# Two-bank projections of a hybrid diffusion layer: token columns cut 320 + 320 where they were cut 384 + 256

## The chip, the cores and the metric

The kernel runs on one core of one Trainium2 chip. The time is device microseconds of one execution. Three runs of the kernel before have a median of 982.79 us (981.87, 982.79, 984.15). The profile is of one execution on the same kind of chip, and lists each instruction by engine: TensorE (PE for the matmuls, PEld for the loads of their weights), VectorE (DVE), ScalarE (ACT), GpSimd (POOL) and SyncE (SP), whose queue issues the transfers.

## The reference

One layer of a bidirectional diffusion backbone is applied to 512 latent and 128 context tokens of 1024 channels. All arithmetic is float32. What matters of it:

```python
h = rms_norm(x, norm_mix_pre) * (1 + sc1) + sh1
proj = h @ w_in                                   # 1024 -> 4640 columns
#   ... Mamba-2 scan in both directions on one part, a 31-tap convolution module on the other
mix = concatenate([y_ssd, u]) @ w_out             # 2048 -> 1024
x = x + g1 * rms_norm(mix, norm_mix_post)
h = rms_norm(x, norm_ffn_pre) * (1 + sc2) + sh2
up = h @ w_ffn_up                                 # 1024 -> 5632
up = dwconv(up)                                   # 3x3 on the latent grid, width 3 on the context
f = (silu(f_gate) * f_val) @ w_ffn_down           # 2816 -> 1024
x = x + g2 * rms_norm(f, norm_ffn_post)
```

The four products with `w_in`, `w_out`, `w_ffn_up` and `w_ffn_down` are the projections. Nearly all of the time goes into them.

## The kernel before

**Layout.** Channels lie on the 128 partitions and tokens along the free dimension: 512 latent tokens and then 128 context tokens, 640 in all (`T`). A projection takes one block of 128 output channels at a time. It sums over blocks of 128 input channels into a tile of PSUM with 1024 float32 columns, which is two banks of 512 (`psum`, `next_ps`, tiles `ps` in the profile; three of them rotate). Small one-bank tiles (`psq`, `pq` in the profile) serve the sums of the norms, the scan and some halves.

**Three products for one.** Weights and inputs are each split into a high part of a reduced float32 format and a remainder (`hi` and `lo`; `wh` and `wl` for weights). `mm3` adds three products for each block of input channels: high weights by high input, high weights by the input's remainder, and the remainder of the weights by high input. 640 columns do not fit into one bank, so each product is two matmuls, one for each half of the tokens, with the same weights, one after the other. Every matmul has its own load of weights. All matmuls of `mm3` are recorded on one line, L415.

**The halves.** `HC` cuts the tokens into 0 to 384 and 384 to 640. `HALF` puts the first half at column 128 of the tile, so that it ends with the first bank at 512, and the second half at column 512. A reader takes both as one stretch of 640 columns through `view`, which begins at column 128.

The same halves order the work around the norms. Before the FFN's first norm and at the end of the kernel, the last output blocks are summed for tokens 0 to 384 first and for 384 to 640 after that, so that the norm of one half runs under the matmuls of the other. In the output projection, blocks 3 to 7 (`OUT_FULL` is 3) go by halves, blocks 0 to 2 take all tokens. In the up projection the first five blocks (`HEAD`) go by halves through `up_mm` (L1259), the other 39 take all tokens through `mm3`. In the down projection block 0 takes all tokens, but its two halves go to two one-bank tiles (`places`); blocks 1 to 6 take all tokens in a two-bank tile; and block 7 goes by halves. All blocks of the input projection take all tokens.

**Order.** The program is recorded as plain Python, and then `issue_in_order` puts each engine's instructions into an order written out as a table of numbers (`ORDER`). The matmuls of a block of output channels therefore mostly stand together on TensorE, but before 540 us two or three blocks, the scan's small matmuls (L744, L807, L818) and the adaLN's (L441, L460) are interleaved.

**What reads the sums.** `out_done` (L1072) adds a stored part to the output projection's sums; `up_conv_of` (L1327 is one call of it) runs a 3x3 convolution of a block on VectorE out of PSUM (L1237); `down_out` (L1407) squares and scales the down projection's sums on ScalarE. In the input projection, ScalarE and VectorE read the tile through `view` as well. Weights come by 512 KB transfers on SyncE's queue, are rounded to `wh` on ScalarE (L311) and their remainder `wl` is made on GpSimd (L313).

Of the kernel before, what the change touches and what calls it, by code (L numbers as in the profile page):

```python
# [11 lines left out]
MUL, ADD, SUB, MAX, MIN = ALU.mult, ALU.add, ALU.subtract, ALU.max, ALU.min  # L12
# [5 lines left out]
T = L + C  # L18
HT = T // 2
HC = ((0, 384), (384, T))  # L20
NCH = T // P
KD = D // P
NPAIR = 8
# [160 lines left out]
def hybrid_layer_kernel(ctx: ExitStack, tc: tile.TileContext, xT, ct, prm, cst, wrest, wdt, idhl_d, wada1, wada2, win,  # L184
                        wout, wup, wdown, st0, yT, nsf, nsb):
    nc = tc.nc
    te, ve, ac, gp, sy = nc.tensor, nc.vector, nc.scalar, nc.gpsimd, nc.sync
# [17 lines left out]
    def nm(s):  # L205
        uid[0] += 1
        return f"{s}_{uid[0]}"


    def slot(tag, dt=F32, shape=(P, T)):  # L210
        if tag in ("H8", "T8"):
            return sb.tile([P, T + 64], dt, tag=tag, name=nm(tag))[:, 48:48 + shape[1]]
        return sb.tile(list(shape), dt, tag=tag, name=nm(tag))
# [4 lines left out]
    def psq(i):  # L218
        return ps.tile([P, 512], F32, tag=f"Q{i}", name=nm(f"pq{i}"))

    def view(t):
        return t[:, 128:128 + T]

    def prm_col(name, i=0, n=1):
        a = _COLS[name][0] + i
        return prms[:, a:a + n]
# [5 lines left out]
    for k in range(KD):  # L232
        t = slot(f"T{k}")
# [147 lines left out]
    ups = [(q, half) for q in range(NF) for half in range(2)]  # L381
# [21 lines left out]
        return hi, lo  # L403

    last_mm = [None]
    HALF = ((128, *HC[0]), (512, *HC[1]))

    def mm3(pt, hi, lo, j, xh, xl, first, last, halves=(0, 1), places=None):
        w1 = hi[:, j * P:(j + 1) * P]
        w2 = lo[:, j * P:(j + 1) * P]  # L410
        for i, (w, x) in enumerate(((w1, xl), (w1, xh), (w2, xh)) if first else ((w1, xh), (w1, xl), (w2, xh))):
            for h in halves:
                o, c0, c1 = HALF[h]
                out = places[h] if places else pt[:, o:o + c1 - c0]
                last_mm[0] = te.matmul(out, w, x[:, c0:c1], start=first and i == 0, stop=last and i == 2)  # L415

# [136 lines left out]
    def proj(n):  # L553
        (u,) = unit_of[n]
        hi, lo = get_unit(u)
        pt = psum(flip[0] % 2)
        flip[0] += 1
        for k in range(KD):
            mm3(pt, hi, lo, k, h_hi[k], h_lo[k], k == 0, k == KD - 1)
        return pt  # L560
# [23 lines left out]
    def chunked(t):  # L584
        return t.rearrange("p (c t) -> p c t", c=NCH)

# [9 lines left out]
    def dtprep():  # L596
# [5 lines left out]
        pd = psq(0)  # L602
        for c in range(NCH):
            te.matmul(pd[:, c * 32:(c + 1) * 32], raw[:, c * P:(c + 1) * P], ids, start=True, stop=True)
        W = NCH * 32
        scr = slot("T9")
        a, n, e, w = (scr[:, i * W:(i + 1) * W] for i in range(4))
        by = lambda t: t.rearrange("p (c h) -> p c h", c=NCH)
        ve.tensor_tensor(by(a), by(pd[:, 0:W]), prm_col("dt_bias", 0, 32).unsqueeze(1).to_broadcast([P, NCH, 32]), ADD)
        ve.scalar_tensor_tensor(n, a, -1.0, a, MUL, MAX)  # L610
        ac.activation(e, n, AF.Exp, scale=-1.0)

        DT = slot("T12")[:, 0:W].rearrange("p (c h) -> p c h", c=NCH)
        ve.tensor_scalar(n, e, 2.0, None, ADD)
# [235 lines left out]
    def gate(p, pg):  # L850
        for (o0, o1), (c0, c1) in UCOLS:
            ac.activation(ub[p % 3][:, o0:o1], view(pg)[:, c0:c1], AF.Tanh, scale=0.5)
# [74 lines left out]
    for it in seq:  # L927
        if it[0] == "proj":
            n = it[1]
            pt = proj(n)  # L930
# [61 lines left out]
    ahead_sb = [None] * KD  # L992
# [45 lines left out]
    def next_ps():  # L1038
        rot[0] += 1
        return psum(rot[0] % 3)  # L1040

    BOTH = (0, 1)
    RANGES = (((0, *HC[0]),), ((0, HC[1][0], L), (1, L, T)))

    def cols_of(halves):
        return slice(HC[halves[0]][0], HC[halves[-1]][1])

    def ranges_of(halves):
        return ((0, 0, L), (1, L, T)) if len(halves) == 2 else RANGES[halves[0]]
# [17 lines left out]
    def out_done(m, halves, pt):  # L1067
        if m_sb[m] is None:
            m_sb[m] = slot(f"M{m}")
        cc = cols_of(halves)  # L1070
        o = m_sb[m][:, cc]
        ve.tensor_tensor(o, view(pt)[:, cc], ahead_sb[m][:, cc], ADD)  # L1072
        if m == 0:
            ac.activation(msq[:, cc], o, AF.Square)
            return
        sq = slot(f"S{16 + m % 2}")
        ac.activation(sq[:, cc], o, AF.Square)
        if m < KD - 1:
            gp.tensor_tensor(msq[:, cc], msq[:, cc], sq[:, cc], ADD)
        else:  # L1080
            sq_last[halves[0]] = sq
# [17 lines left out]
    def xr_fetch():  # L1099
        for k in range(KD):  # L1100
            t = slot(f"T{8 + k}")
            sy.dma_start(t[:, slice(*HC[0])], xT[:, k, slice(*HC[0])])
            xr[0].append(t[:, slice(*HC[0])])

# [28 lines left out]
    class Mid:  # L1133
        def __init__(self, half):
            self.half, (self.c0, self.c1) = half, HC[half]
            self.n = self.c1 - self.c0
            self.t = {}
# [70 lines left out]
    for half in range(2):  # L1208
        for m in range(OUT_FULL, KD):
            pt = next_ps()  # L1210
# [14 lines left out]
    def up_conv(v, i, out):  # L1225
        w = lambda a, b: prm_col("ffn_w", 9 * i + 3 * a + b)
        ac.activation(out, v, AF.Identity, bias=prm_col("ffn_b", i), scale=w(1, 1))  # L1227
        vl = v[:, 0:L].rearrange("p (r c) -> p r c", c=GW)
        ol = out[:, 0:L].rearrange("p (r c) -> p r c", c=GW)
        for a in range(3):  # L1230
            for b in range(3):
                if (a, b) == (1, 1):
                    continue
                r0, r1 = max(0, 1 - a), min(ROWS, ROWS + 1 - a)
                q0, q1 = max(0, 1 - b), min(GW, GW + 1 - b)
                ob = ol[:, r0:r1, q0:q1]
                ve.scalar_tensor_tensor(ob, vl[:, r0 + a - 1:r1 + a - 1, q0 + b - 1:q1 + b - 1],  # L1237
                                        w(a, b), ob, MUL, ADD)
        ve.scalar_tensor_tensor(out[:, L + 1:T], v[:, L:T - 1], w(1, 0), out[:, L + 1:T], MUL, ADD)
        return ve.scalar_tensor_tensor(out[:, L:T - 1], v[:, L + 1:T], w(1, 2), out[:, L:T - 1], MUL, ADD)  # L1240
# [4 lines left out]
    for i in range(KD // 2):  # L1245
        t = sb.tile([P, 2, HC[1][1] - HC[1][0]], F32, tag=f"H{i}", name=nm("xr"))
        sy.dma_start(t, xT[:, 2 * i:2 * i + 2, slice(*HC[1])])
        xr[1] += [t[:, 0, :], t[:, 1, :]]
    head = [next_ps() for i in range(3)]
# [6 lines left out]
    def up_mm(i, k, half, pt, o):  # L1256
        (hi, lo), (c0, c1) = ws[i], HC[half]
        for j, (w, x) in enumerate(((hi, h2[k][0]), (hi, h2[k][1]), (lo, h2[k][0]))):
            te.matmul(pt[:, o:o + c1 - c0], w[k] if i in (1, 2) else w[:, k * P:(k + 1) * P], x[:, c0:c1],  # L1259
                      start=k == 0 and j == 0, stop=k == KD - 1 and j == 2)  # L1260
        if k == KD - 1 and i >= 3:
            ac.activation(raws[i][:, c0:c1], pt[:, o:o + c1 - c0], AF.Copy)
# [48 lines left out]
    def up_conv_of(i, v, out):  # L1311
        conved[i] = out
        prior[0] = up_conv(v, ups[i][1] * NF + ups[i][0], out)

    acc_slot = lambda q, half: slot({(1, 0): "S16", (2, 1): "S17"}.get((q, half), f"S{10 + 2 * half + q % 2}"))
    ada_half(6, ada_w2)
    for i in (0, 3, 4, 1, 2):
        if i >= 3:
            pt = psq((i + 1) % 2)
            for k in range(KD):  # L1320
                up_mm(i, k, 1, pt, 0)
            horizon[0] += 1
            fetch(horizon[0])
            continue
        for k in range(KD):
            up_mm(i, k, 1, head[i], 512)
        up_conv_of(i, view(head[i]), acc_slot(*ups[i]))  # L1327
    horizon[0] = None
    FRAW = [f"H{i}" for i in (2, 3, 4, 7, 0, 1, 8, 9, 10, 11, 12, 13, 14, 15, 5, 6)] + ["S8", "S9"]

# [11 lines left out]
    for i in range(HEAD, 2 * NF):  # L1342
        q, half = ups[i]
        w = get_unit(unit_of["up", i])
        pt = next_ps()
# [56 lines left out]
    def down_out(m, half, pt):  # L1402
        halves = BOTH if half is None else (half,)
        if mg[m] is None:
            mg[m] = slot(mtags[m])
        cc = cols_of(halves)
        v = zero_at[half] if m == 0 else view(pt)[:, cc]  # L1407
        if m == 0:
            ac.activation(msq[:, cc], v, AF.Square)
        else:  # L1410
            sq = sq_last[0] if half else slot("AT" if m % 2 else "HL")
            ac.activation(sq[:, cc], v, AF.Square)
            if half is None:
                gp.tensor_tensor(msq[:, cc], msq[:, cc], sq[:, cc], ADD)
            else:
                sq_last[half] = sq
        for c, c0, c1 in ranges_of(halves):
            ac.activation(mg[m][:, c0:c1], v[:, c0 - cc.start:c1 - cc.start], AF.Copy, scale=gg2[:, m, c:c + 1])
# [32 lines left out]
    zero_at = [psq(h)[:, 0:HC[h][1] - HC[h][0]] for h in range(2)]  # L1451
# [7 lines left out]
    for m in range(2, KD - 1):  # L1459
        pt = next_ps()  # L1460
        down_mm(m, None, pt, range(NF))
        down_out(m, None, pt)

    m = KD - 1
    pt = next_ps()
    down_mm(m, 0, pt, range(NF))
    down_out(m, 0, pt)
    pt = next_ps()
# [128 lines left out]
```

## Time and profile before

| | |
|---|---|
| median of three runs | 982.79 us |
| span of the profiled execution | 979.4 us |
| TensorE busy (7623 matmuls) | 944.5 us, 96% |
| weight loads busy (7623) | 920.9 us, 94% |
| VectorE, ScalarE, GpSimd busy | 686.9, 471.3, 577.9 us |
| matmuls of L415 | 5424: 2712 of 384 columns, 2712 of 256 |
| mean granted TensorE clock | 0.996 of full speed |
| moved from and to memory | 117.5 MB, mean 120 GB/s |

The page gives the profiled execution's span, from its first to its last instruction; it does not give that execution's time from the outside. A matmul's duration in the profile (332 to 337 ns for 384 columns, 279 to 282 for 256) is longer than the distance to the start of the next one, because matmuls overlap in the pipeline. What a stream of matmuls costs is read from the starts, or from a stretch of the chain of waits with its count. Rows of the timeline merge successive matmuls on the same tiles whatever their width, and name the width of the first.

### The profile page before, as it was taken

To read this page: it belongs to the slowest core of one execution; us is meant where nothing else is said; L and a number is where in the kernel's file an instruction comes from. 1 tells how busy PE (TensorE), PEld (TensorE's weight loads), DVE (VectorE), ACT (ScalarE), POOL (GpSimd) and SP (SyncE) were. 2 spreads that over 40 slices of the span, in tenths; PEclk is the share of its full clock that TensorE was granted. 3 is DMA by queue.
4 is the path that set the end of the run, shared out by engine and by line. 5 is a ranking of instruction groups with operands and counts; after the bars stand their busy time and mean duration, and the time that the engine had idled before them with its cause. 6 is when DMAs were issued, how large, how long until landed. Compare 5 with 4: busy or idle time off the path is not lost.

```text
span 979.4 us, 18795 instructions
## 1 busy us (share of the span) xinstructions
PE 944.5 (96%) x7623; PEld 920.9 (94%) x7623; DVE 686.9 (70%) x1076; ACT 471.3 (48%) x799; POOL 577.9 (59%) x416
## 2 busy tenths in 40 slices
PE   4999999999999999999999999999999999999995
PEld 3799999999999998998889999999999999999995
DVE  1769898999989997523585998998988898400004
ACT  4355666877668477622464852323232336322211
POOL 1334699889999882534662994444454436543434
PEclk9999999999999999999999999999999999999998
DMA  9622424433424422578662322222222231322213
GB/s 347 250 72 86 117 82 127 146 95 123 139 80 142 128 91 93 196 244 303 200 218 88 129 86 69 84 78 73 86 66 86 66 87 54 94 69 76 82 38 108
DMA packets 50294, 117.52 MB, mean 120 GB/s; under 512 B 6016, under 2 KB 13952, under 8 KB 50208
## 3 DMA queue, kind: packets, MB, share of 16 engines
q1 hardware_dynamic: 50208, 116.33, 37.2%
q8 instruction: 60, 0.98, 0.4%
q14 instruction: 26, 0.21, 0.1%
HBM read 112.55 MB, written 3.75 MB: 119 GB/s over the span
## 4 chain that ended last, share of the span: by engine, by line
PE 87%; DMA 3%; ACT 3%; DVE 2%; SPq 1%; POOL 1%; issue 1%; POOLq 0%; ACTq 0%; DVEq 0%
PE ps L415 72%; PE ps L1259 3%; PE pq L415 2%; PE pq L818 2%; PE pq L807 1%; PE pq L460 1%; SPq L452 1%; DMA wr<-in_wout 1%; PE pq L744 1%; PE pq L441 1%; POOL wl L313 1%; PE pq L473 1%; DMA S<-acD 1%; ACT wh L311 1%; DMA T<-in_wada 1%
## 5 line engine op out<-in xcount | busy, mean ns | idle before, releaser
L313 POOL TENSOR_TENSOR wl<-wr,wh 128x1024 fp32r<-128x1024 f32 (+3 forms) x127 | 290.4, 2290 | 316.3 <-ACT wh L311 299.2
L415 PE MATMUL ps<-H,wh 128*128 128x384 f32 (+1 forms) x1636 | 315.7, 309 | 0.1
L311 ACT ACTIVATE wh<-wr 128x1024 fp32r<-128x1024 f32 (+3 forms) x131 | 131.3, 1003 | 316.2 <-PE ps L415 183.2
L415 PE MATMUL ps<-T,wh 128*128 128x384 f32 (+1 forms) x1472 | 272.5, 306 | 1.8 <-ACT S L1227 1.8
L1237 DVE SCALAR_TENSOR_TENSOR S<-ps,prms,S 128x441 f32<-128x441 f32 (+2 forms) x336 | 233.5, 695 | 29.4 <-ACT S L1227 18.9
L415 PEld LDWEIGHTS ps<-H,wh 128*128 128x128 f32 x1636 | 249.0, 188 | 2.7 <-issue 1.7
L415 PEld LDWEIGHTS ps<-T,wh 128*128 128x128 f32 x1472 | 218.9, 188 | 2.2 <-ACT S L1227 2.1
L872 DVE SCALAR_TENSOR_TENSOR ps<-u,prms,ps 128x655 f32<-128x655 f32 x205 | 185.1, 903 | 10.8 <-ACT ps L869 4.8
L415 PE MATMUL ps<-H,wl 128*128 128x384 f32 (+1 forms) x818 | 191.8, 309 | 0.0
L415 PE MATMUL ps<-T,wl 128*128 128x384 f32 (+1 forms) x736 | 166.2, 305 | 0.0
L415 PEld LDWEIGHTS ps<-H,wl 128*128 128x128 f32 x818 | 129.0, 188 | 1.0 <-issue 1.0
L415 PEld LDWEIGHTS ps<-T,wl 128*128 128x128 f32 x736 | 113.0, 188 | 0.0
L488 DVE RECIPROCAL rsm<-rsm 128x160 f32<-128x160 f32 (+2 forms) x9 | 7.4, 817 | 147.1 <-ACT rsm L487 147.1
L415 PE MATMUL ps<-S,wh 128*128 128x384 f32 (+1 forms) x420 | 88.0, 310 | 1.6 <-ACT wh L311 1.6
L415 PEld LDWEIGHTS ps<-S,wh 128*128 128x128 f32 x420 | 66.5, 188 | 2.8 <-ACT wh L311 1.8
L415 PE MATMUL ps<-S,wl 128*128 128x384 f32 (+1 forms) x210 | 54.9, 309 | 0.3 <-POOL wl L313 0.3
L789 ACT ACTIVATE S<-S,AC 128x128 f32<-128x128 f32 x140 | 45.5, 392 | 2.4 <-DMA S<-acD 2.4
L885 POOL TENSOR_TENSOR T<-T,T 128x640 f32<-128x640 f32 x20 | 32.0, 1602 | 12.5 <-ACT T L881 12.5
L1227 ACT ACTIVATE S<-ps,prms 128x640 f32<-128x640 f32 x42 | 36.5, 869 | 0.0
L415 PEld LDWEIGHTS ps<-S,wl 128*128 128x128 f32 x210 | 35.2, 188 | 0.9 <-POOL wl L313 0.5
L881 ACT ACTIVATE T<-u,prms 128x512 f32<-128x512 f32 (+1 forms) x54 | 27.9, 554 | 6.8 <-POOL T L885 6.8
L1339 POOL TENSOR_TENSOR H<-S,S 128x640 f32<-128x640 f32 x16 | 25.3, 1581 | 0.0
(346 smaller groups left out, 1180.3 us busy)
## 6 DMA issues: line engine op xcount, KB each, us to landing
wr<-in_wup SPq DMA_DIRECT2D x44, 512.0 KB, 3.5
wr<-in_win SPq DMA_DIRECT2D x36, 512.0 KB, 3.9
T<-in_wada SPq DMA_DIRECT2D x49, 256.0 KB, 5.4
S<-acD SPq DMA_DIRECT2D x28, 320.0 KB, 4.7
wr<-in_wdown SPq DMA_DIRECT2D x16, 512.0 KB, 3.4
wr<-in_wout SPq DMA_DIRECT2D x13, 512.0 KB, 4.5
H<-in_wada SPq DMA_DIRECT2D x23, 256.0 KB, 4.6
S<-in_wada SPq DMA_DIRECT2D x16, 256.0 KB, 5.4
```

The costliest lines, as they stand in the source:

```text
L311: ac.activation(hi[:, :n], raw[:, :n], AF.Copy)
L313: lo_eng.tensor_tensor(lo[:, :n], raw[:, :n], hi[:, :n].bitcast(F32), SUB)
L415: last_mm[0] = te.matmul(out, w, x[:, c0:c1], start=first and i == 0, stop=last and i == 2)
L789: ac.activation(rc, rc, AF.Relu, scale=-1.0, bias=AC2[:, c, row:row + 1])
L818: te.matmul(py[64 * h:64 * h + 64, i * P:(i + 1) * P], xt[:, c * P + 64 * h:c * P + 64 * h + 64], rs[h, d][:, c * P:(c + 1) * P], start=d ...
L872: ve.scalar_tensor_tensor(acc, u[:, j:j + UO], w(j), acc, MUL, ADD)
L881: ac.activation(t[:, b:c], u[:, a:a + c - b], AF.Copy, scale=w(j))
L885: gp.tensor_tensor(far, far, t, ADD)
L1227: ac.activation(out, v, AF.Identity, bias=prm_col("ffn_b", i), scale=w(1, 1))
L1237: ve.scalar_tensor_tensor(ob, vl[:, r0 + a - 1:r1 + a - 1, q0 + b - 1:q1 + b - 1], w(a, b), ob, MUL, ADD)
L1259: te.matmul(pt[:, o:o + c1 - c0], w[k] if i in (1, 2) else w[:, k * P:(k + 1) * P], x[:, c0:c1], start=k == 0 and j == 0, stop=k == KD - 1 ...
L1339: gp.tensor_tensor(f_raw[q], a, b, MUL)
```

## The change

Where `mm3` sums all tokens in one two-bank tile, it cuts the 640 columns into 0 to 320 and 320 to 640. The first half is put at column 192, so that it still ends with the first bank, and the second at 512 (`EVEN`). `view` begins at 192 for such a tile and at 128 for one that is summed by halves; its callers say which. Tiles that are summed by halves, the one whose halves go to two one-bank tiles, and `up_mm` keep 384 and 256. The norms' halves (`HC`) stay.

```diff
 HC = ((0, 384), (384, T))
+HALF = ((128, *HC[0]), (512, *HC[1]))
+EVEN = ((512 - T // 2, 0, T // 2), (512, T // 2, T))
...
-    def view(t):
-        return t[:, 128:128 + T]
+    def view(t, even=True):
+        o = EVEN[0][0] if even else HALF[0][0]
+        return t[:, o:o + T]
...
-    HALF = ((128, *HC[0]), (512, *HC[1]))

     def mm3(pt, hi, lo, j, xh, xl, first, last, halves=(0, 1), places=None):
         w1 = hi[:, j * P:(j + 1) * P]
         w2 = lo[:, j * P:(j + 1) * P]
+        cuts = EVEN if len(halves) == 2 and not places else HALF
         for i, (w, x) in enumerate(((w1, xl), (w1, xh), (w2, xh)) if first else ((w1, xh), (w1, xl), (w2, xh))):
             for h in halves:
-                o, c0, c1 = HALF[h]
+                o, c0, c1 = cuts[h]
                 out = places[h] if places else pt[:, o:o + c1 - c0]
                 last_mm[0] = te.matmul(out, w, x[:, c0:c1], start=first and i == 0, stop=last and i == 2)
...
-        ve.tensor_tensor(o, view(pt)[:, cc], ahead_sb[m][:, cc], ADD)
+        ve.tensor_tensor(o, view(pt, len(halves) == 2)[:, cc], ahead_sb[m][:, cc], ADD)
...
-        up_conv_of(i, view(head[i]), acc_slot(*ups[i]))
+        up_conv_of(i, view(head[i], False), acc_slot(*ups[i]))
...
-        v = zero_at[half] if m == 0 else view(pt)[:, cc]
+        v = zero_at[half] if m == 0 else view(pt, len(halves) == 2)[:, cc]
```

The order of instructions stays the same on every engine, and so do the waits between them. On TensorE, 4830 of the 5424 matmuls of `mm3` get another width: 2415 of 384 and 2415 of 256 columns become 4830 of 320. One place in the up projection, the first blocks of input channels of one block of outputs (`ps0` is the PSUM tile, `T` are inputs, `wh77` and `wl77` the weights' two parts; the size is partitions by columns), before:

```order
L415 MATMUL ps0_705_7018<-T8_600_5820,wh77_6825 128x384
L415 MATMUL ps0_705_7018<-T8_600_5820,wh77_6825 128x256
L415 MATMUL ps0_705_7018<-T0_599_5819,wh77_6825 128x384
L415 MATMUL ps0_705_7018<-T0_599_5819,wh77_6825 128x256
L415 MATMUL ps0_705_7018<-T0_599_5819,wl77_6827 128x384
L415 MATMUL ps0_705_7018<-T0_599_5819,wl77_6827 128x256
```

and after the change (two matmuls of one row now have the same size):

```order
L418 MATMUL ps0_705_7018<-T8_600_5820,wh77_6825 128x320 x2
L418 MATMUL ps0_705_7018<-T0_599_5819,wh77_6825 128x320 x2
L418 MATMUL ps0_705_7018<-T0_599_5819,wl77_6827 128x320 x2
L418 MATMUL ps0_705_7018<-T1_602_5824,wh77_6825 128x320 x2
L418 MATMUL ps0_705_7018<-T9_603_5825,wh77_6825 128x320 x2
```

The line moved from 415 to 418 by the lines that were added above it; tiles, weights and order are those of before.

## Prediction

> **What bounds the kernel now.** I read the chain of waits first, then the busy time by stage, then the idle time of TensorE, and last the timeline of single matmuls, since the change alters nothing but their width.
>
> The chain that ended last, cut to 600 to 960 us:
>
> ```profile
> by line: PE ps L415 94.6%; PE pq L415 5.3%; PE pq L473 0.2%
> 599.99 207.20 PE ps L415 x1443
> 846.87 112.60 PE ps L415 x771
> ```
>
> From 600 to 960 us nothing but the matmuls of `mm3` (L415) ends the work: 1443 of them follow each other for 207.20 us without a gap, 143.6 ns each, and two of them (a pair of 384 and 256 columns) take 287.2 ns. Busy time by stage (TensorE, weight loads, VectorE, ScalarE, GpSimd, granted clock, DMA) says the same, and how it was earlier:
>
> ```profile
> 50.00:150.00 100.00, 99.31 (x702) 98.69 (x699) 86.80 (x134) 60.28 (x113) 61.81 (x44) 1.00 0.29 87
> 250.00:350.00 100.00, 99.91 (x822) 98.17 (x821) 93.11 (x125) 65.33 (x133) 88.47 (x85) 1.00 0.41 125
> 450.00:550.00 100.00, 93.04 (x979) 88.12 (x978) 62.00 (x135) 53.33 (x102) 58.03 (x40) 1.00 0.60 199
> 850.00:950.00 100.00, 100.00 (x695) 100.00 (x693) 0.00 (x0) 24.25 (x34) 43.84 (x23) 1.00 0.25 73
> ```
>
> TensorE is taken nearly the whole time in every stage, at a granted clock of 1.00, and only around 450 to 550 us does it wait for more than a per cent or two. What TensorE waits for, over the whole span, is short:
>
> ```profile
> PE pq L473 <- ACT S L498: 11.7, 3, 5.5
> PE pq L460 <- DMA T<-in_wada: 2.2, 4, 1.0
> PE ps L415 <- ACT S L1227: 1.8, 1, 1.8
> PE ps L415 <- ACT wh L311: 1.6, 1, 1.6
> ```
>
> So the time is the number of matmuls times the distance from one start to the next, and a busy TensorE hides nothing of a change to that distance. In the chain, the long unbroken stretches before 540 us are
>
> ```profile
> 57.78 35.20 PE ps L415 x244
> 115.92 14.13 PE ps L415 x96
> 196.52 18.79 PE ps L415 x129
> 289.41 16.46 PE ps L415 x111
> 306.41 16.98 PE ps L415 x116
> ```
>
> together 101.56 us for 696 matmuls: 145.9 ns each, 291.8 a pair. The same pair is dearer there than after 600 us, and the timeline of TensorE shows two patterns (a row merges matmuls of the same tiles; x2 is one pair, x4 two):
>
> ```profile
> 120.66 0.76 PE L415 MATMUL ps<-H,wh 128*128 128x384 f32 x4
> 121.25 0.46 PE L415 MATMUL ps<-H,wl 128*128 128x384 f32 x2
> 121.56 0.76 PE L415 MATMUL ps<-H,wh 128*128 128x384 f32 x4
> 602.54 0.33 PE L415 MATMUL ps<-T,wl 128*128 128x384 f32 x1
> 602.71 0.28 PE L415 MATMUL ps<-T,wl 128*128 128x256 f32 x1
> 602.83 0.33 PE L415 MATMUL ps<-T,wh 128*128 128x384 f32 x1
> 603.00 0.45 PE L415 MATMUL ps<-T,wh 128*128 128x256 f32 x2
> ```
>
> At 602 us the starts are 0.17 us apart after 384 columns and 0.12 after 256 (the starts have two decimals; with the 287.2 of the long stretch this is 168 to 169 and 118 to 119). At 120.66 to 121.56 us three pairs take 0.90 us: 300 a pair. I call them the **short** and the **long pattern**. The stretches before 540 us mix them, the later ones are nearly all short.
>
> **The change part by part.** The rewritten offset of the consumers' view (192 instead of 128) moves no instruction: each reader takes the same 640 columns over two banks as before. No wait, transfer or order changes. What changes is the width of 4830 of the 5424 matmuls of L415: 2415 pairs of 384 + 256 become 320 + 320. The tile `m = 0` of the down projection and the tiles summed by halves keep their widths. Where the 2415 lie, by the busy time of L415 alone in a window (matmuls, weight loads):
>
> ```profile
> 540.00:960.00 420.00, 415.18 (x2872) 414.65 (x2872) 1.00 0.25 76
> ```
>
> Of these 2872, 132 are `m = 0` (22 blocks, three products, two halves), 66 the first half of the last tile, and about 14 belong to its second half or were in flight at 540: 2660 are left, 1330 pairs. The other 1085 pairs lie before 540 us.
>
> The columns to stream are the same, 640 a pair, and so is the number of weight loads. A gain or loss can only come from what a matmul takes beyond its columns. No row shows 320 columns of this type, so the cost is bounded from both sides by rows of equal widths in succession. Such rows exist, where a tile is summed by halves. The last tile, first half, 384 columns 66 times (22 blocks, three products, so 65 steps from its first start to its last):
>
> ```profile
> 946.67 0.51 PE L415 MATMUL ps<-S,wh 128*128 128x384 f32 x2
> ...
> 958.08 0.34 PE L415 MATMUL ps<-H,wl 128*128 128x384 f32 x1
> ```
>
> 11.41 us over 65 steps is **175.5 ns**: 7 more than the same width takes where it alternates with 256 in the short pattern. And 256 columns in succession, in the output projection:
>
> ```profile
> 486.24 0.28 PE L415 MATMUL ps<-S,wh 128*128 128x256 f32 x1
> 486.36 0.28 PE L415 MATMUL ps<-H,wl 128*128 128x256 f32 x1
> 486.48 0.40 PE L415 MATMUL ps<-S,wh 128*128 128x256 f32 x2
> 486.71 0.28 PE L415 MATMUL ps<-S,wl 128*128 128x256 f32 x1
> 486.83 0.28 PE L415 MATMUL ps<-S,wh 128*128 128x256 f32 x1
> 486.95 0.28 PE L415 MATMUL ps<-H,wh 128*128 128x256 f32 x1
> 487.07 0.28 PE L415 MATMUL ps<-S,wl 128*128 128x256 f32 x1
> ```
>
> Seven steps in 0.83 us: **118.6 ns**, as much as in the alternation. One of each in succession costs 175.5 + 118.6 = 294.1, while the alternating pair costs 287.2 in the short pattern: streams of equal widths do not get the short 384. After the change every pair is a stream of equal widths. Halfway between the two rows lies 320: 147.05 ns, **294.1 a pair**. This is the value I take, because these are the only rows in which a matmul follows one of its own width.
>
> Its ends: from the lower row with the smallest slope a row gives, (168.5 - 118.5) / 128 = 0.39 ns a column within the short pattern, 118.6 + 64 x 0.39 = 143.6 (287.2 a pair); from the upper row with the same slope, 175.5 - 25 = 150.5 (301). Without a tie to the equal-width rows, the lowest conceivable is 384's best step shrunk in proportion, 168.5 x 320 / 384 = 140.4 (280.8).
>
> The sum by 294.1: after 540 us 1330 x (294.1 - 287.2) = 9.2 us; before it 1085 x (294.1 - 291.8) = 2.5 us; together **+11.7 us**. The cover for it would be TensorE's own waits, in which a slower stream swallows time it now idles. For L415 these are the few us quoted above, and none after 600 us, where most of the loss lies; I take nothing off.
>
> The execution on the page has a span of 979.4 us. The runs shown have a median of 982.79, so 3.4 us lie around the span if the profiled run was an ordinary one. Span forecast 979.4 + 11.7 = 991.1, time 982.8 + 11.7 = **994.5 us**.
>
> The Trainium skill, page "TensorE: Matmul & The Clock Gate", section "Back-to-back issue gap", gives a warm matmul N/2.4 + 2.5 ns, and the section "LDWEIGHTS" 107 ns for a load of 128 columns, which 256 streamed columns just cover. By that rule, as an estimate, either cut costs 271.7 ns a pair and the change is worth 0 us. The trace does not agree on the size (287.2 and 300 a pair, 175.5 for 384 in succession against 162.5 by the rule), and shows that what comes on top depends on the neighbour.
>
> **The rivals.**
>
> *Weight load as a floor (ends on the other side: faster).* Each matmul needs its own weight load, which runs under the one before. Narrow matmuls do not get shorter with their width: of the sums' spread, eight of 96 columns and then the next tile's start:
>
> ```profile
> 962.21 1.03 PE L481 MATMUL pq<-rsm,csts 128*128 128x96 f32 x8
> 963.02 0.49 PE L415 MATMUL ps<-T,wh 128*128 128x256 f32 x2
> ```
>
> 0.81 us for eight, 101 ns each, for a width at which 256's step would shrink to 44. A floor of 101 or more is close to 256's 118.5, so part of that step may be the load and not the stream. Then 384 + 256 wastes what 256 falls short of, and 320, well over the floor, streams at 384's best price: between 140.4 (in proportion) and 143.4 (slope of the short pattern), say 141.9, 283.8 a pair. Price: 1330 x 3.4 + 1085 x 8.0 = 13.2 us less, **969.6 us**. It decides wherever 320 takes under 144.6 ns, half of today's mean pair, (1330 x 287.2 + 1085 x 291.8) / 2415 = 289.3. Against it: 384 in succession is also over the floor and takes 175.5, not 168.5.
>
> *The short pattern everywhere.* The pair keeps 287.2, and equal widths cannot fall into the long one. Then only the stages before 540 gain: 1085 x 4.6 = 5.0 us, **977.8 us**. For it: both patterns exist for the same tiles, so the long one is no property of the columns. Against it: the same rows of equal width.
>
> *A fixed surcharge for each matmul, whatever its width and neighbour:* the pair costs what it did, **982.8 us**. For it: the number of matmuls and columns is unchanged. Against it: 168.5 and 175.5 for the same 384 columns. That the change doesn't do what it says can be left out of account, since the widths stand in the instructions.
>
> *The long pattern everywhere,* 300 a pair: 1330 x 12.8 + 1085 x 8.2 = 25.9 us, **1008.7 us**.
>
> **How the numbers follow.** About 0.2%, 2 us, is what a measurement can tell from no change (the three runs span 981.87 to 984.15). Equal widths as the equal-width rows have it: 0.54; weight floor 0.18; short pattern 0.12; fixed surcharge 0.12; long pattern 0.04. Slower 0.58, same 0.12, faster 0.30. The likeliest case alone has 986 to 1003 (290.5 to 297.5 a pair, half of the way to its ends). The range has to reach the weight floor, since the signs differ: 968 to 1006 leaves out its lower part and most of the long pattern, about 0.15.
>
> **What would show it.** In the timeline after 600 us, the rows of x2 of the same tiles should start 0.294 us after each other where they started 0.287 apart; the unbroken stretch of L418 that answers to 600 to 807 us should show 147 ns for each matmul in place of 143.6. Stages 550 to 960 us should lose some 9 us, those before 540 a quarter of that. The halves' rows (175.5 and 118.6) must stay. I am wrong if 320 after 320 takes under 144.6: at 142 the floor was the weight load, at 143.6 the short pattern holds for equal widths too; and wrong in another way if the matmuls are unchanged in distance and the time moves through a wait of L418 on another engine.

## The result

| | before | 320 + 320 |
|---|---|---|
| median of 4 runs each | 982.53 us (981.87 to 984.15) | 995.41 us (993.35 to 996.39) |
| ratio, 95% interval | | 1.0127 (1.0111 to 1.0144) |
| span of the profiled execution | 979.4 us | 991.3 us |

The changed kernel is slower by 12.9 us; the span grew by 11.9. The forecast was 994.5 us, with a span of 991.1.

The profile of the changed kernel, read as that of before: the chain of waits from 600 us on (a stretch begins at the first figure, lasts the second, and counts its matmuls),

```profile
by line: PE ps L418 94.3%; PE pq L418 5.1%; PE pq L484 0.2%; PE pq L476 0.2%; DVE H L1449 0.2%; ACT HL L1440 0.1%; PE pq L426 0.0%; issue 0.0%; ACTq L1440 0.0%
600.44 215.06 PE ps L418 x1467
855.80 114.69 PE ps L418 x771
```

and the same long stretch before, in the chain of the whole span:

```profile
596.53 210.67 PE ps L415 x1467
```

The 1467 matmuls are the same in both and follow each other without a gap. They take 146.6 ns each instead of 143.6, 293.2 a pair instead of 287.2. This one stretch is the measure of every experiment below; in all profiles TensorE has its full clock throughout it. With it the time is placed: the stretch begins 3.9 us later than before (600.44 against 596.53), gains 4.4 us itself (215.06 - 210.67), 0.6 until the next long stretch begins (855.80 against 846.87), and 2.1 in that one (114.69 - 112.60). The last 0.9 us come after it. The unbroken stretches before 540 us, with the counts of before:

```profile
59.39 35.84 PE ps L418 x244
118.14 14.08 PE ps L418 x96
198.57 18.92 PE ps L418 x129
292.22 16.48 PE ps L418 x111
309.25 17.00 PE ps L418 x116
```

102.32 us for 696 matmuls: 294.0 a pair, where it was 291.8. Of the 0.76 us more, 0.64 lie in the first of the five; the other four, which held long pairs before, changed by 0.13 or less. There is one pattern now, in every stage: rows of two pairs and of one pair, at 121 us and at 650 us,

```profile
121.06 0.75 PE L418 MATMUL ps<-H,wh 128*128 128x320 f32 x4
121.65 0.46 PE L418 MATMUL ps<-H,wl 128*128 128x320 f32 x2
121.94 0.75 PE L418 MATMUL ps<-H,wh 128*128 128x320 f32 x4
...
649.97 0.75 PE L418 MATMUL ps<-T,wh 128*128 128x320 f32 x4
650.56 0.46 PE L418 MATMUL ps<-T,wl 128*128 128x320 f32 x2
650.85 0.60 PE L418 MATMUL ps<-T,wh 128*128 128x320 f32 x3
```

with three pairs in 0.88 us in both places. No wait on another engine took up or added any of this: the four largest sums of TensorE's waits are 12.1, 1.8, 1.6 and 1.6 us, where they were 11.7, 2.2, 1.8 and 1.6.

### The profile page after: what moved, and what is told of

It reads as the page before. It is cut to its first block, busy times and chain, and to the rows that moved or that the text cites. A ratio compares the mean times of both kernels' runs of the same rounds, so it can differ in the third digit from the quotient of the medians.

```text
span 991.3 us, 18795 instructions
## 1 busy us (share of the span) xinstructions
PE 956.3 (96%) x7623; PEld 932.1 (94%) x7623; DVE 688.2 (69%) x1076; ACT 470.9 (48%) x799; POOL 574.5 (58%) x416
## 4 chain that ended last, share of the span: by engine, by line
PE 87%; DMA 5%; ACT 3%; DVE 2%; SPq 1%; POOL 1%; issue 1%; POOLq 0%; ACTq 0%; DVEq 0%
PE ps L418 73%; PE ps L1262 3%; PE pq L418 2%; DMA T<-in_wada 2%; PE pq L821 2%; PE pq L810 1%; PE pq L463 1%; SPq L455 1%; DMA wr<-in_wout 1%; PE pq L747 1%; DMA S<-acD 1%; DMA S<-in_wada 1%; PE pq L444 1%; ACT wh L314 1%; PE pq L484 1%
## 5 line engine op out<-in xcount | busy, mean ns | idle before, releaser
L418 PE MATMUL ps<-H,wh 128*128 128x320 f32 (+2 forms) x1636 | 318.5, 311 | 0.0
L418 PE MATMUL ps<-T,wh 128*128 128x320 f32 (+2 forms) x1472 | 276.7, 309 | 1.8 <-ACT S L1230 1.8
L418 PEld LDWEIGHTS ps<-H,wh 128*128 128x128 f32 x1636 | 258.9, 188 | 2.8 <-issue 1.7
L418 PEld LDWEIGHTS ps<-T,wh 128*128 128x128 f32 x1472 | 231.3, 188 | 2.1 <-ACT S L1230 2.1
L418 PE MATMUL ps<-H,wl 128*128 128x320 f32 (+2 forms) x818 | 193.2, 310 | 0.0
L418 PE MATMUL ps<-T,wl 128*128 128x320 f32 (+2 forms) x736 | 168.7, 308 | 0.0
L418 PEld LDWEIGHTS ps<-H,wl 128*128 128x128 f32 x818 | 138.2, 188 | 1.0 <-issue 1.0
L418 PEld LDWEIGHTS ps<-T,wl 128*128 128x128 f32 x736 | 123.3, 188 | 0.0
L418 PE MATMUL ps<-S,wh 128*128 128x320 f32 (+2 forms) x420 | 88.8, 312 | 1.6 <-ACT wh L314 1.6
L418 PE MATMUL ps<-S,wl 128*128 128x320 f32 (+2 forms) x210 | 55.3, 310 | 0.6 <-POOL wl L316 0.6
```

## The experiments

The theory that went on trial is the one behind the chosen term: the distance from a matmul to the next depends on its width and on the width of the one before it, and only a 384 after a 256 is short. Against it stood the place of the halves, the order of the banks, and the weight load. Runs of the kernel before on the same chip stand beside each. The first view quoted is always the chain of waits, with the stretch of 1467 matmuls (a pair is its length by 1467, times two); steps of single widths are means over the starts in the trace from 600 to 810 us.

### The narrow half first: 256 + 384

```diff
-EVEN = ((512 - T // 2, 0, T // 2), (512, T // 2, T))
+CUT = 256
+EVEN = ((512 - CUT, 0, CUT), (512, CUT, T))
```

> The cut of the two-bank tiles is 256 + 384 instead of 320 + 320: the narrow half first, at tokens 0 to 256 and columns 256 to 512 of the tile, the wide one at columns 512 to 896. Every place in PSUM and every offset into the input differs from the kernel before, the alternation of widths is the same. Theory of the neighbour (a matmul's step depends on its own width and on that of the one before it; 384 after 256 is short, a width after its like is not): 168 to 169 and 118 to 119 ns after 600 us, pairs of 287, time within 3 us of the kernel before, 980 to 986. Rival, the place (the first half's start at column 192 of its bank, or the second half's start 320 columns into the input, costs the 6 ns a pair): this cut too has other places, so pairs of about 293 and 992 to 997 us.

```profile
598.09 210.70 PE ps L419 x1467
```

981.63 us, ratio 0.9987 (0.9973 to 1.0001). 287.3 a pair, the stretch of the kernel before to 0.03 us, though every half lies elsewhere in PSUM and in the input. The place of the halves is not the cause.

### 384 + 256 with the halves of every second product swapped

```diff
-            for h in halves:
+            for h in (halves[::-1] if len(halves) == 2 and not places and (3 * j + i) % 2 else halves):
```

> The kernel before with 384 + 256 at their old places, but every second product takes its halves in the other order: 384 256 | 256 384 | 384 256. Half of all widths now follow their like, nothing else differs. Neighbour: half of the 384 take 175.5 and half 168.5, the 256 stay at 118.6, so 290.6 a pair; after 540 us 1330 pairs x 3.4 = 4.5 us more than before, before 540 us no change, time 985 to 990. Rival, the place: every half lies where it lay in the kernel before, so 287 a pair and 982 to 983 us.

```profile
602.89 216.15 PE ps L415 x1467
```

997.0 us, ratio 1.0132 (1.0106 to 1.0158): 294.7 a pair, more than 320 + 320. Both expectations missed. 256 stayed at 118 ns in either neighbourhood and 384 after 384 took 175.4, as forecast, but 384 after 256 took 177 and not 168.5. A narrower matmul ahead is therefore not enough to make the 384 short. The short pattern needs the strict alternation; with the order turned in every second product, it is gone for all of them.

### 320 + 320 with the halves of every second product swapped

The same line in the changed kernel.

> The changed kernel (320 + 320) with the halves of every second product in the other order. Widths still follow their like; two successive matmuls now go to the same bank every second time, and the input's two halves swap order. Neighbour: 146.6 ns each, 995 us, no difference from the changed kernel. Rival, the banks (alternating banks at equal widths is what costs, or what saves): a change of 2 us or more against the changed kernel.

```profile
600.13 215.06 PE ps L418 x1467
```

992.78 us, ratio 1.0107 (1.0069 to 1.0144). The stretch is the changed kernel's to the digit. Which bank follows which does not matter for the stretch at 320 + 320, and the total agrees with the changed kernel's within its scatter.

### 352 + 288

`CUT = 352`.

> The cut is 352 + 288: unequal, alternating, and the narrow one is wider than 256. Neighbour, if inequality alone gives the short step: 352 after 288 is short, the pair keeps 287 as 384 + 256, time 980 to 984. Neighbour, if the step shrinks in proportion to the difference of widths (64 instead of 128): pairs of about 290, 987 to 990 us. Rival, the weight load (only 256, close to the floor of 101 to 112 ns that narrow matmuls show, gives the next matmul a lead): 288 is well over the floor, so the pair behaves as 320 + 320, 293 and 994 to 996 us.

```profile
602.75 215.15 PE ps L419 x1467
```

994.07 us, ratio 1.0107 (1.0083 to 1.013): 293.3 a pair, 162.7 and 130.6 ns. The widths alternate and differ by 64, and the pair costs what two equal ones cost. The rival's number came out (the weight load's; whether its reason holds too, the narrow weights below show), and both forms of the neighbour theory fell: 320 + 320 has no penalty for being equal. The kernel before had an advantage that 352 + 288 lacks as well.

### The change in the FFN alone

```diff
-        cuts = EVEN if len(halves) == 2 and not places else HALF
+        cuts = EVEN if late[0] and len(halves) == 2 and not places else HALF
...
     x2 = m_sb
+    late[0] = True
```

and `view` asks `late[0]` too.

> Only the FFN's two-bank tiles (up and down projection, from about 540 us on) are cut 320 + 320; the input and output projection keep 384 + 256. In the traces of the two kernels the stretch after 540 us grew by 7.8 us and the part before it by about 3. If the loss is the distance between matmuls and nothing else, the parts add: 320-wide steps of 146.6 ns after 540 us, the two patterns of the kernel before ahead of it, time 990 to 992 us. Rival (part of the loss before 540 us comes from what the changed order of finishing does to other engines, or the late loss is carried over from the early part): under 988 or over 994 us.

```profile
596.82 215.06 PE ps L420 x1467
```

991.02 us, ratio 1.0095 (1.0072 to 1.0118). The stretch starts within 0.3 us of the kernel before, and then is the changed kernel's. The loss after 540 us is local: it arises where the widths are changed, without anything carried over from the early part. It is 9.9 us of the 12.9; the change in the early part alone was not run.

### Weights of half the width, 320 + 320 and 384 + 256

```diff
                 out = places[h] if places else pt[:, o:o + c1 - c0]
+                if not (first and i == 0) and not (last and i == 2):
+                    out, w = out[0:64], w[:, 0:64]
```

in the changed kernel,

> The changed kernel (320 + 320) with weights of 64 output channels instead of 128 in all products of a block but its first and its last, in mm3. Output channels 64 to 127 of each block thus get only two of the products, which leaves part of the sum out. Columns streamed and number of matmuls are the same; a weight load covers 64 columns instead of 128. Theory of the load (the 13 ns that a step of 320 takes over its columns come from the weight load that runs beside the stream): steps fall from 146.6 to 140 or less. Rival, the matmul itself (the surcharge has nothing to do with how much is loaded): 146 to 147 as before.

and in the kernel before:

> The kernel before (384 + 256) with the same narrowing of the weights to 64 output channels in all but a block's first and last product. Theory of the load: both patterns vanish, 256 falls to 113 or less and 384 to 168 or less everywhere, pairs of 280 or less, and the pair costs the same as in the 320 + 320 kernel with narrow weights. Rival, the matmul itself: short pairs of 287 and some long ones of 300, as in the kernel before, so 6 ns under 320 + 320.

One execution of each; these two kernels leave part of the sum out. The chain and, by groups with mean ns, the weight loads; first 320 + 320 (985.37 us):

```profile
595.54 213.33 PE ps L420 x1467
```

```profile
L420 PEld LDWEIGHTS ps<-T,wh 128*64 128x64 f32 x1394 | 186.7, 134 | 15.3
L420 PEld LDWEIGHTS ps<-H,wl 128*128 128x128 f32 x112 | 19.1, 188 | 1.1 <-issue 0.3
```

then 384 + 256 (983.62 us):

```profile
594.16 213.51 PE ps L417 x1467
```

A load took 134 ns instead of 188, so it was 54 ns shorter. The step of 320 fell only from 146.6 to 145.4, so the load's length does not set it. In 384 + 256 the 256 fell from 118.4 to 117.0, so it was no floor set by the load either. But the short 384 held in one product of three only: of 717 steps after 384 columns between 601 and 810 us, 240 take 169 or 170 ns and the others 173 to 178. The mean is 174 in every stage, and the pair costs 291.1, 3.9 more than with full weights, while 320 + 320 came to 290.8. With the narrower weights the two cuts cost the same, as the load theory said, though at 291 and not at 280. So most of the advantage of 384 + 256 is lost with them, while the bulk of the step stays. The narrowing shortens the load and also halves the output channels that a matmul writes; which of the two matters was not separated.

### 416 + 224, 400 + 240 and 368 + 272

`CUT = 416`, `400`, `368`, one execution of each.

> The cut is 416 + 224: alternating and more unequal than before. If unequal widths make the short pattern, and only 352 + 288 was not unequal enough: 416 + 224 at 287 a pair or less, time 980 to 984. If 384 + 256 is one lucky meeting of widths: 293 a pair as with 320 + 320 and 352 + 288, 994 to 996. If the weight load is a floor for the narrow one (101 to 112 ns or more, where 224 would take 104 by the slope of the equal-width rows, 0.44 ns a column): 189 + 112 = 301 a pair or more, over 1005 us.

> The cut is 400 + 240. The second half now begins 64 bytes off a multiple of 128 in every tile but the shifted ones. Theory of the pattern (pairs come to whole steps of 6.67 ns, 293.3 where no special rhythm is found): 293 to 300 a pair, 994 to 1010 us. Rival (the narrow one near a weight load's length leads to a short wide one, at 240 as at 256): 287 a pair, 980 to 985 us.

> The cut is 368 + 272, between the kernel before and 352 + 288; the second half again begins 64 bytes off a multiple of 128. Theory of the pattern: 293 to 300 a pair, 994 to 1010 us. Rival (the narrow one near a weight load's length): 287 to 290 a pair, 980 to 989 us.

416 + 224:

```profile
609.02 223.85 PE ps L419 x1467
```

400 + 240:

```profile
601.35 216.52 PE ps L419 x1467
```

368 + 272:

```profile
603.19 216.57 PE ps L419 x1467
```

1014.87, 995.64 and 997.76 us: 305.2, 295.2 and 295.3 a pair. In 416 + 224 the forecast of the load as a floor is the one that was met (301 or more, over 1005 us), but not by its working: 224 columns take 99.4 ns, below the 101 to 112 that I had taken for a floor, and 416 then takes 205.7, where 189 was to be expected by the slope of the equal widths; what the narrow one saves, the next one pays, and more. The reason is open. At 400 + 240 and 368 + 272 the second halves also begin 64 bytes off a multiple of 128, which those of the other cuts do not, so these two do not separate width from that. Of the seven cuts run, 384 + 256 in its two orders is the only one below 293; the nearest cuts without such an offset are 352 + 288 and 416 + 224. None of the versions beats the kernel before by more than its interval.

### The shifted tiles

Two of the input tiles, H8 and T8, lie 48 columns into a wider tile. Without it:

```diff
-            return sb.tile([P, T + 64], dt, tag=tag, name=nm(tag))[:, 48:48 + shape[1]]
+            return sb.tile([P, T + 64], dt, tag=tag, name=nm(tag))[:, 0:shape[1]]
```

in the kernel before,

> The kernel before (384 + 256), with the input tiles H8 and T8 laid 192 bytes earlier, like all other input tiles (the code lays them 48 columns into a wider tile; its reads then begin 64 bytes off a multiple of 128). In the trace of the kernel before, most stretches of the long pattern end at the block's first matmul on H8 or T8. Theory of the pattern (287 and 300 a pair are two rhythms of the same work, and what sets one of them is the last disturbance): without the shift a block that has fallen into the long pattern stays in it until something else disturbs it; over 192 pairs at 300 before 540 us, and after 600 us, where nothing else disturbs the stream, one rhythm throughout: 986 to 1003 us if it is the long one, 979 to 982 if it is the short one. Rival (the distance is set by the width and the widths around it alone): the patterns stand as before, and about 1.3 us are saved for 48 blocks that no longer begin on the shifted tile, 981 to 982.5.

and in the changed one:

> The changed kernel (320 + 320) with the same tiles unshifted. Theory of the pattern: 320 + 320 has only the one mean of 146.6 ns that it shows everywhere, so nothing to be thrown into or out of; 146.6 remains, time 993 to 996. Rival (146.6 is itself one of two rhythms, held by the shifted tile): another mean, 143.3 or 150, in some or all blocks, and 3 us or more away from the changed kernel.

384 + 256 unshifted, two rows of the chain:

```profile
289.90 16.77 PE ps L415 x111
600.60 210.27 PE ps L415 x1467
```

320 + 320 unshifted:

```profile
597.99 215.16 PE ps L418 x1467
```

983.58 us, ratio 0.9997 (0.9982 to 1.0011), and 992.18 us, ratio 1.0105 (1.0077 to 1.0133). In 384 + 256 two things happened. The long pattern ran on past the tile that used to end it: the stretch at 290 us, with 20 long pairs in a row before and 43 now, grew from 16.46 to 16.77 us, which is 23 pairs by 13 ns. And the stretch after 600 us, short throughout, lost 0.40 us: 13 ns for each of its 30 blocks. Before 540 us, 274 pairs take about 300 ns (297 to 304), where 192 did. The two work against each other, and the time does not move beyond its interval. So the patterns are states that the stream keeps until something disturbs it, but the stream after 600 us stayed short without help; the expectation had left open which of the two it would be. In 320 + 320 the shift makes no difference of size, 0.10 us in 215, and 146.6 is not one of two.

## Why the prediction was right

**The sign, the time and the mechanism's place.** TensorE bounds, nothing covers its stream, and the distance between matmuls decides: all of this held. The stretch of 1467 and the change in the FFN alone show the loss where the widths changed.

**The terms.** The pair was put at 294.1 and measured at 293.2 (late) and 294.0 (early). After 540 us 9.2 us were forecast. From 597 us on 7.1 appeared (4.4 + 0.6 + 2.1), and about 0.9 more between 540 and 597 (some 155 pairs by 6.0), 8.0 in all: the value was 0.9 ns a pair too high there. Of the 3.9 us by 597 us this leaves 3.0, and 1.4 of these were there at 29 us, where the first long row of `mm3` begins. The chains before and after:

```profile
28.82 5.50 PE ps L415 x37
30.20 5.42 PE ps L418 x37
```

Of these 1.4 us, 1.0 arises between 24 and 28.5 us (the same matmuls start 0.4 us later at the one and 1.4 at the other), where the changed kernel's clock was granted at half for one stretch of 3.41 us (25.29 to 28.70) and that of the kernel before was not. The windows of the first 50 us, before and after, have the granted clock third from the end, 1.00 and 0.97:

```profile
0.00:50.00 50.00, 35.76 (x463) 27.55 (x463) 23.41 (x49) 20.46 (x31) 10.67 (x22) 1.00 0.80 293
0.00:50.00 50.00, 34.94 (x439) 27.04 (x439) 23.44 (x49) 20.18 (x30) 9.39 (x22) 0.97 0.81 293
```

That is no effect of the widths. Four other profiles have the same half clock there, among them 256 + 384, whose time is that of the kernel before, and in them the matmuls fall back by 0.7 to 1.2 us over the same place; in the eight without it they fall back by 0.1 or less. For the early term 1.6 us are left, forecast at 2.5. The remaining 0.9 us arise at the very end, from the clock too (below).

**The luck.** The two terms of the sum came to 9.6 us in this profile, where 11.7 were forecast, and 2.3 us of its span's 11.9 are outside the sum, 1.9 of them the clock. That the span was met to 0.2 us is luck. The same 320-wide stretch cost 9.8 us over the kernel before in the swapped order (992.78 against 983.02) and 8.3 without the shifted tiles (992.18 against 983.91).

**The step that failed: "streams of equal widths do not get the short 384".** The two rows of equal widths gave the right number by interpolation, but the reason I drew from them is not the cause. Equality is no cost (352 + 288 takes 293.3), and a narrower matmul ahead is no gain by itself (384 after 256 took 177 in the swapped order). What the runs put in its place: about 293 a pair, or 294 to 295, is what this stream takes at 320 + 320, 352 + 288, 368 + 272, 400 + 240 (these two with the offset of 64 bytes) and in the swapped 384 + 256; 416 + 224 takes 305. The kernel before, after 600 us, was the exception at 287.2, found throughout only at 384 + 256 in strict alternation and with full weights. The change did not add a cost, it gave up that exception. Before 540 us the exception already held only in part, mixed with a pattern of 300, and so less was lost there.

**The rivals.** The weight load as a floor of the 256 is out: 54 ns less load took 1.4 ns off it. The short pattern did not hold for equal widths, and the long one appeared in no 320-wide stretch. The fixed surcharge was nearer the truth than its 0.12: but for the exception, the cost of a pair did not depend on how 640 columns are cut between 400 + 240 and 320 + 320, to within 2 ns; for the kernel before it is wrong by 6, and for 416 + 224 by 12.

**What stays open** is why 384 + 256 falls into the short pattern. The swapped order shows that it needs the alternation, the narrow weights that most of it goes with a shorter load or fewer output channels, the unshifted tiles that it persists once entered; none of the runs shows what in TensorE makes it, nor why 416 + 224 falls out on the other side.

## What to carry to other kernels

Where TensorE's stream is the time, the cost of a matmul is no property of its width: read it from the starts in a gapless stretch, in the very sequence of widths that will run, and judge a new cut by one such stretch, which resolves 0.1 us in 215 where the total of a run scatters by 3 and more. Look at the granted clock of every window before a difference of a microsecond is given to the change. Rows of a similar sequence (here, halves summed alone) gave the size of an untried one to 1 ns here although the reason read into them was not the cause, but that makes them a measurement to interpolate and no rule to extend. That a narrow matmul looks close to the length of its weight load is no reason to widen it; a shorter load has to show first that the load holds it up.

## What the runs showed of the hardware

**Three lengths of a pair, 6.67 ns apart.** Without the shifted tiles the gapless stretch takes 210.27 / 1467 x 2 = 286.7 ns a pair with 384 + 256 and 215.16 / 1467 x 2 = 293.3 with 320 + 320; the long pattern takes 300. They are 43, 44 and 45 times 6.67. This is no rule for every stream: 290.8 and 291.1 with narrow weights, 294.7 in the swapped order, 295.2 and 305.2 at other cuts are no multiples. A tile whose reads begin 192 bytes later costs 13 ns a block in the short pattern (0.40 us for 30 blocks), and nothing at 320 + 320 (215.06 with it, 215.16 without).

**A clock at half speed at the end.** The last 0.9 us of the longer span is this: the final spread of the norm's sums, eight matmuls, took 1.12 us before and 1.99 after. The chain of the changed kernel, and its windows (span, TensorE, weight loads, VectorE, ScalarE, GpSimd, granted clock, DMA share, GB/s):

```profile
973.39 0.88 PE pq L484 x8
981.19 1.99 PE pq L484 x8
```

```profile
979.00:981.00 2.00, 0.32 (x8) 0.16 (x8) 1.97 (x4) 1.11 (x4) 2.00 (x2) 1.00 0.54 194
981.10:983.20 2.10, 1.97 (x8) 1.78 (x8) 0.45 (x2) 0.00 (x1) 1.25 (x1) 0.50 0.58 208
```

Before the change the same eight ran at full clock:

```profile
970.10:971.30 1.20, 1.10 (x8) 0.97 (x8) 0.43 (x2) 0.00 (x0) 1.18 (x1) 1.00 0.52 188
```

What TensorE does ahead of them is the same in both: the halves' matmuls end 2.3 us earlier, eight small matmuls follow, and then comes a gap of 1.46 us. The difference is the moment at which the clock falls. In the traces' records of the granted clock it is 981.02 us after the change, ahead of the eight, and 971.90 before it, after their end. Of the other profiled runs, nine had 1.12 us there and three 1.17 to 1.74; in these three the clock falls while the eight run. In all 14 profiles, every stretch between two changes of the clock lasts a whole multiple of 3.413 us (3.41, 6.83 and 952.32 are 1, 2 and 279 times). The Trainium skill, page "TensorE: Matmul & The Clock Gate", section "What's actually happening", says that the clock is set by windows of 3413 ns that run freely; the stretches agree with it. The section also says that it falls after an idle window; here the longest gap between matmuls in the 3.41 us ahead of 981.02 was 1.3 us, so on this the trace does not agree. A difference of up to 0.9 us at the end of two profiles of this kernel can be the clock alone.
